# Seven-product feed-forward up-projection: PSUM copies issued ahead of the last pair's activations, another home for the first weights, one weight's subtraction on DVE

## The chip, the cores and the metric

The kernel runs on one core of one Trainium2 chip. The metric is the device time of the whole program in microseconds (us), median of three runs. Engines are named as in the profile: PE (TensorE matmuls) and PEld (its weight loads), DVE (VectorE), ACT (ScalarE), POOL (GpSimd), SP (SyncE, which here issues the loads). ACTq and SPq are DMA issues in the queues of ACT and SP.

## The reference

One decoder block: two token mixers, a merge, and a gated feed-forward with a convolution over three tokens. The change lies in the first half of the feed-forward, `h @ w_up`, the convolution and the gate; T = 1024 tokens, 1024 features, 2 x 2816 columns.

```python
def conv_ffn(h, w_up, conv_w, conv_b, w_down):
    u = h @ w_up
    T = u.shape[1]
    up = jnp.pad(u, ((0, 0), (CONV_WIDTH - 1, 0), (0, 0)))
    u = sum(up[:, i:i + T] * conv_w[i] for i in range(CONV_WIDTH)) + conv_b
    gate, val = jnp.split(u, 2, axis=-1)
    return (jax.nn.gelu(gate, approximate=True) * val) @ w_down
```

## The kernel before

The up-projection goes by 22 pairs of column tiles: a pair is 128 gate columns (weight tile j, channel b = 0) and the 128 value columns that they gate (tile j + 22, b = 1), for two halves of 512 tokens (hf = 0, 1). The first three pairs are made in the plain way by `up_std`. The other 19 (n = 0 to 18) are made by seven products of half the depth in place of eight: sums of weight halves times sums of input halves, put together after. Every product is three float32r terms (high x high, high x low, low x high) over four blocks of 128, so 12 matmuls of 512 columns; a pair is 84 matmuls. For the first four pairs (n < 4) two of the seven products are made ahead, in a stage called "e" here (lines 1108 to 1117), stored to DRAM (`e_s` to `e_d`) and loaded again; such a pair is 60 matmuls.

A pair's products in PE's order, with the PSUM tile: X1 (`ps_x`), Z1 (`ps_z`), T1 (`ps_t`), Y (`ps_y`), X2 (`ps_x`, accumulated onto X1), Z2 (`ps_z`, onto Z1), T2 (`ps_t`, onto T1). Between them: ACT copies X1 to `s1` (L1183) and Z1 to `s5` (L1188); DVE adds T1 into `s5` (L1190) and Y into `s1` (L1192); ACT copies X2 into `ub` (L1195), POOL adds `s1` and `s5` into `ub` (L1196), DVE adds Z2 (L1198) and T2 (L1200) with `s1` into `ub`. X2 may not start before the copy of X1, Z2 not before that of Z1, T2 not before the add of T1.

The weights of a pair: SP loads two tiles of 512 KB (`st1` L1148, `st2` L1150; both are `w_st` in the profile). DVE forms sums: `w_sa` (two operations, L1163 and L1164) and, in place, one half each of `st2` (L1166) and `st1` (L1167). `cut` makes of a weight its high part, a cast on ACT (L1159), and its low part, the weight minus the high part (L1160), on POOL for w1, w2 and w3 and on DVE for w4. w1 is cut from `st1`, w2 from `w_sa`, w3 from the two halves made in place, w4 from the untouched half of `st2`; the subtraction for w4 is the last reader of an `st2` buffer, of which there are two.

Then the convolution and the gate, for each token half: `conv` is one ACT operation (L1063) and two DVE operations (L1064, L1066) for each channel, `gate` a GELU on ACT (L1071), a product on DVE (L1072) and a store from ACT's queue (L1073).

Each engine works through its own queue in order. What order that is, a scheduler decides when the program is built, from the order of the code, from priorities (`tc.high_priority` for the weights) and from its own estimates. Weight buffers come from pools: `wp` lives from early on; `wx` and `fp` are opened when the "e" stage's pools (`b12`, `es`, `w3s`) are closed, in the same memory.

Of the kernel before, what the change touches and what calls it, by code (L numbers as in the profile page):

```python
# [9 lines left out]
F32 = mybir.dt.float32  # L10
F32R = mybir.dt.float32r
# [13 lines left out]
FT = 22  # L25
# [133 lines left out]
def body(tc, nc, xT, xN, pos, wch, wbrw, wbret, wout, wup, wdn, w2a2, gw2, rows, vecs, consts0, consts1, out):  # L159
    V, S, G, PE = nc.vector, nc.scalar, nc.gpsimd, nc.tensor  # L160
    ctx = ExitStack()

    @contextmanager
    def tile_pool(**kw):
        with tc.tile_pool(**kw) as pool:
            yield Lines(pool)

    with ctx:
# [30 lines left out]
        pool_lo = [False]  # L199
        wpools = [(wp, (2, 3, 2))]  # L200

        def load_w(src, kt, full=None, hi=None, lo=None, st=None):

            wp, nb = wpools[cnt[0] % len(wpools)]
            with tc.high_priority(offset=WPRIO if cnt[0] > 3 else 0):
                if st is None:
                    st = wp.tile([128, full or kt, 128], F32, tag="ws", name="w_st", bufs=nb[0])[:, 0:kt, :]
                nc.sync.dma_start(st, src)
            with tc.high_priority(offset=WPRIO if cnt[0] > 1 else 0):
                if hi is None:  # L210
                    hi = wp.tile([128, full or kt, 128], F32R, tag="wh", name="w_hi", bufs=nb[1])[:, 0:kt, :]
                S.copy(hi, st)  # L212
                if lo is None:
                    lo = wp.tile([128, full or kt, 128], F32R, tag="wl", name="w_lo", bufs=nb[2])[:, 0:kt, :]
                cnt[0] += 1
                eng = V if (cnt[0] % 3 == 0 and not pool_lo[0]) or cnt[0] < 3 else G
                eng.tensor_tensor(out=lo, in0=st, in1=hi, op=ALU.subtract)  # L217
            return hi, lo

# [819 lines left out]


        bp = ctx.enter_context(tile_pool(name="bp", bufs=1, reuse_waits="tile"))
        ectx = ExitStack()
        b12 = ectx.enter_context(tile_pool(name="b12", bufs=1, reuse_waits="tile"))
        es = ectx.enter_context(tile_pool(name="es", bufs=2, reuse_waits="tile"))

        w3s = ectx.enter_context(tile_pool(name="w3s", bufs=1, reuse_waits="tile"))
        wpools[:] = [(wp, (2, 3, 2)), (w3s, (1, 1, 1)), (wp, (2, 3, 2))]
        f_d = dp.tile([2, FT, 128, 512], F32, name="f_d")
        carry = cp.tile([128, 2 * NSTD, 2], F32, name="carry", bufs=1)
# [24 lines left out]

        def up_std(j, hf, late=False):
            cv = []
            ws = [load_w(wup[j + FT * b], 8) for b in range(2)]
            pss = [big("ps_up") for b in range(2)]
            if late:

                for b in range(2):
                    for k in range(8):
                        for z in range(2):
                            PE.matmul(pss[b], ws[b][z][:, k, :], hn2[hf][k][0], start=k + z == 0, stop=False)
                for b in range(2):
                    for k in range(8):
                        PE.matmul(pss[b], ws[b][0][:, k, :], hn2[hf][k][1], start=False, stop=k == 7)
            for b in range(2):
                w, ps = ws[b], pss[b]
                if not late:  # L1090
                    mm3(ps, [(w[0][:, k, :], w[1][:, k, :], hn2[hf][k][0], hn2[hf][k][1]) for k in range(8)])
                ub = es.tile([128, 514], F32, tag=f"ub{b}", name="ub")
                if hf == 0:
                    G.memset(ub[:, 0:2], 0.0)
                else:
                    G.tensor_copy(ub[:, 0:2], carry[:, 2 * j + b, :])
                S.copy(ub[:, 2:514], ps)
                if hf == 0:
                    G.tensor_copy(carry[:, 2 * j + b, :], ub[:, 512:514])
                cv.append(conv(es, ub, b, j, ps))  # L1100
            gate(j, hf, *cv)
# [6 lines left out]
        for n0 in range(0, NEAR, 2):  # L1108
            ws = [load_w(wup[NSTD + n], 8) for n in (n0, n0 + 1)]
            pss = [big("ps_e") for n in range(2)]  # L1110
            for z in range(2):
                for n in range(2):
                    mmb(pss[n], ws[n], range(4 * z, 4 * z + 4), hn2[0][4 * z:4 * z + 4], z == 0, True)
                    t = es.tile([128, 512], F32, tag=f"u{z}", name="e_s")
                    S.copy(t, pss[n])
                    nc.scalar.dma_start(e_d[n0 + n, z], t)
        up_std(0, 1, True)
# [24 lines left out]
        W8 = [128, 8, 128]  # L1142
        lh, rh_ = slice(0, 4), slice(4, 8)

        for n, j in enumerate(range(NSTD, FT)):
            with tc.high_priority(offset=WPRIO):
                st1 = wp.tile(W8, F32, tag="ws", name="w_st", bufs=2)
                nc.sync.dma_start(st1, wup[j])  # L1148
                st2 = wx.tile(W8, F32, tag="ws", name="w_st", bufs=2)
                nc.sync.dma_start(st2, wup[j + FT])  # L1150
                sa = wx.tile(W8, F32, tag="sa", name="w_sa")
                if n >= NEAR:
                    w1 = wp.tile(W8, F32R, tag="wh", name="w_hi", bufs=3), wx.tile(W8, F32R, tag="wl", name="w_lo", bufs=3)
                w2 = wx.tile(W8, F32R, tag="wh", name="w_hi", bufs=2), wx.tile(W8, F32R, tag="wl", name="w_lo", bufs=3)
                w3 = wp.tile(W8, F32R, tag="wh", name="w_hi", bufs=3), wp.tile(W8, F32R, tag="wl", name="w_lo", bufs=2)
                w4 = wx.tile(W8, F32R, tag="wh", name="w_hi", bufs=2), wp.tile(W8, F32R, tag="wl", name="w_lo", bufs=2)

                def cut(w, ks, src, eng):
                    S.copy(w[0][:, ks, :], src)  # L1159
                    eng.tensor_tensor(out=w[1][:, ks, :], in0=src, in1=w[0][:, ks, :], op=ALU.subtract)  # L1160
                if n >= NEAR:
                    cut(w1, slice(0, 8), st1, G)
                V.tensor_tensor(out=sa[:, lh, :], in0=st2[:, lh, :], in1=st2[:, rh_, :], op=ALU.add)  # L1163
                V.tensor_tensor(out=sa[:, rh_, :], in0=st1[:, lh, :], in1=st2[:, lh, :], op=ALU.subtract)  # L1164
                cut(w2, slice(0, 8), sa, G)
# [144 lines left out]
```

## Time and profile before

| | us |
|---|---|
| median of 3 runs | 1898.92 (1895.99 to 1899.91) |
| the profiled execution | 1902.93 |
| its span, first to last instruction | 1901.1 |
| the stretch from the "e" stage to the first product of n = 0 | about 1180 to 1254 |
| the seven-product stage, n = 0 to 18 | about 1254 to 1625 |

Times in the rows below are microseconds from the start of the span. A row of the timeline gives start, duration, engine, line, operation, tiles written and read, and in brackets how long the engine sat idle before it and what released it.

### The profile page before, as it was taken

The page shows a single profiled execution, that of the slowest core. Times are in us where ns is not written, and L with a number is a line of the kernel's source. Part 1 is how long each engine was busy: PE and PEld are TensorE (multiplying, and loading weights), DVE is VectorE, ACT ScalarE, POOL GpSimd, SP SyncE. Part 2 cuts the span into 40 slices and gives each one's busy share as a digit, 9 for nine tenths or more (in the row PEclk, how much of TensorE's full clock was granted, in tenths as well). Part 3 has the DMA queues.
Part 4 walks back from the last instruction along what each step waited for, and adds up shares of the span by engine and source line. Part 5 has one row for each costly group of instructions (what it writes and reads, how often), then busy time and mean ns, then how long its engine had stood idle before and what let it go on. Part 6 is the DMA issues. An engine that isn't in the chain of part 4 may idle for free.

```text
span 1901.1 us, 27394 instructions
## 1 busy us (share of the span) xinstructions
PE 1787.9 (94%) x10610; PEld 1450.2 (76%) x10610; DVE 1176.8 (62%) x2067; ACT 649.7 (34%) x993; POOL 686.1 (36%) x492
## 2 busy tenths in 40 slices
PE   8779999999999999999999999888999999999996
PEld 7657778788777778878788777666777777777885
DVE  4786584755666635663445828689888888752413
ACT  6543212111111112332443434544444444443320
POOL 1344523312212221111564744535454454222523
PEclk9989999999999999999999999899999999999998
DMA  8333532433333225455643735332222222664521
GB/s 285 87 113 100 191 83 67 134 90 94 109 100 105 69 89 176 151 177 172 217 154 123 242 106 197 122 135 89 89 67 78 83 73 78 221 210 142 188 92 44
DMA packets 202690, 244.44 MB, mean 129 GB/s; under 512 B 60992, under 2 KB 136256, under 8 KB 201536
## 3 DMA queue, kind: packets, MB, share of 16 engines
q1 hardware_dynamic: 125712, 171.11, 29.4%
q10 hardware_dynamic: 76848, 71.59, 11.5%
q8 instruction: 83, 1.36, 0.3%
q14 instruction: 47, 0.39, 0.1%
HBM read 177.10 MB, written 65.54 MB: 128 GB/s over the span
## 4 chain that ended last, share of the span: by engine, by line
PE 51%; DVE 17%; DMA 9%; issue 5%; ACT 4%; POOL 4%; ACTq 0%; SPq 0%; DVEq 0%; POOLq 0%
PE ps_side L224 7%; PE ps_side L223 7%; PE ps_side L225 7%; DVE u_f L1064 4%; PE ps_dn L225 3%; PE ps_dn L223 3%; PE ps_dn L224 3%; POOL w_lo L1160 2%; DMA w_st<-in_wup_dram 2%; DVE w_sa L1164 2%; DVE w_sa L1163 2%; PE ps_o L224 1%; PE ps_o L225 1%; PE ps_o L223 1%; DVE u_f L1066 1%
## 5 line engine op out<-in xcount | busy, mean ns | idle before, releaser
L217 POOL TENSOR_TENSOR w_lo<-w_st,w_hi 128x1024 fp32r<-128x1024 f32 (+2 forms) x112 | 272.4, 2433 | 513.6 <-ACT w_hi L212 183.8
L212 ACT CAST w_hi<-w_st 128x1024 fp32r<-128x1024 f32 (+2 forms) x162 | 161.7, 999 | 403.6 <-PE ps_side L224 125.8
L224 PE MATMUL ps_side<-hnl,w_hi 128*128 128x512 f32 x640 | 256.3, 400 | 0.0
L223 PE MATMUL ps_side<-hnh,w_hi 128*128 128x512 f32 x640 | 255.6, 399 | 0.0
L225 PE MATMUL ps_side<-hnh,w_lo 128*128 128x512 f32 x640 | 254.8, 398 | 0.0
L223 PEld LDWEIGHTS ps_side<-hnh,w_hi 128*128 128x128 f32 x640 | 121.1, 189 | 26.8 <-issue 1.5
L225 PEld LDWEIGHTS ps_side<-hnh,w_lo 128*128 128x128 f32 x640 | 121.1, 189 | 26.2 <-issue 0.8
L224 PEld LDWEIGHTS ps_side<-hnl,w_hi 128*128 128x128 f32 x640 | 121.0, 189 | 26.3 <-issue 1.5
L217 DVE TENSOR_TENSOR w_lo<-w_st,w_hi 128x1024 fp32r<-128x1024 f32 (+1 forms) x50 | 64.0, 1280 | 83.7 <-ACT w_hi L212 41.5
L1064 DVE SCALAR_TENSOR_TENSOR u_f<-ub,vct,u_f 128x512 f32<-128x512 f32 x88 | 105.5, 1204 | 13.9 <-ACT u_f L1063 13.8
L1160 POOL TENSOR_TENSOR w_lo<-w_st,w_hi 128x512 fp32r<-128x512 f32 (+1 forms) x53 | 106.0, 2024 | 0.0
L1063 ACT ACTIVATE u_f<-ub,vct 128x512 f32<-128x512 f32 x76 | 59.9, 812 | 129.2 <-DVE ub L1198 110.8
L223 PE MATMUL ps_rw<-hnh,w_hi 128*128 128x512 f32 (+1 forms) x224 | 87.8, 392 | 13.2 <-ACT hnh L288 7.0
L224 PE MATMUL ps_rw<-hnl,w_hi 128*128 128x512 f32 (+1 forms) x224 | 86.7, 387 | 0.7 <-DVE hnl L289 0.7
L225 PE MATMUL ps_rw<-hnh,w_lo 128*128 128x512 f32 (+1 forms) x208 | 80.0, 385 | 0.0
L225 PE MATMUL ps_b<-y_hi,w_lo 128*128 128x512 f32 x192 | 75.1, 392 | 1.9 <-DVE w_lo L217 1.2
L223 PE MATMUL ps_b<-y_hi,w_hi 128*128 128x512 f32 x192 | 75.2, 392 | 0.7 <-ACT w_hi L212 0.6
L224 PE MATMUL ps_b<-y_lo,w_hi 128*128 128x512 f32 x192 | 74.8, 390 | 0.0
L223 PE MATMUL ps_dn<-f_k,w_hi 128*128 128x512 f32 (+1 forms) x198 | 72.5, 366 | 0.0
L225 PE MATMUL ps_dn<-f_k,w_lo 128*128 128x512 f32 (+1 forms) x198 | 72.4, 367 | 0.0
L224 PE MATMUL ps_dn<-f_k,w_hi 128*128 128x512 f32 (+1 forms) x198 | 72.2, 366 | 0.0
L223 PE MATMUL ps_z<-b_hi,w_hi 128*128 128x512 f32 x152 | 60.4, 397 | 12.2 <-ACT w_hi L1159 8.0
(418 smaller groups left out, 4342.2 us busy)
## 6 DMA issues: line engine op xcount, KB each, us to landing
w_st<-in_wup_dram SPq DMA_DIRECT2D x54, 512.0 KB, 3.6
w_st<-in_wch_dram SPq DMA_DIRECT2D x52, 512.0 KB, 4.0
w_st<-in_wdn_dram SPq DMA_DIRECT2D x38, 512.0 KB, 4.0
pj_d<-ot ACTq DMA_DIRECT2D x64, 256.0 KB, 2.2
zvg<-pj_d SPq DMA_DIRECT2D x8, 1536.0 KB, 9.2
f_d<-u_f ACTq DMA_DIRECT2D x44, 256.0 KB, 2.1
L<-L_d SPq DMA_DIRECT2D x8, 1344.0 KB, 6.0
w_st<-in_wbret_dram SPq DMA_DIRECT2D x16, 512.0 KB, 3.7
```

Source lines behind the costliest of these rows:

```text
L212: S.copy(hi, st)
L217: eng.tensor_tensor(out=lo, in0=st, in1=hi, op=ALU.subtract)
L223: PE.matmul(ps, wh, xh, start=first and a == 0, stop=False, skip_group_check=skip)
L224: PE.matmul(ps, wh, xl, start=False, stop=False, skip_group_check=skip)
L225: PE.matmul(ps, wl, xh, start=False, stop=last and a == n - 1, skip_group_check=skip)
L1063: S.activation(u, src, AF.Identity, bias=VC("cb")[:, i:i + 1], scale=VC("cw2")[:, i:i + 1])
L1064: V.scalar_tensor_tensor(out=u, in0=ub[:, 1:513], scalar=VC("cw1")[:, i:i + 1], in1=u, op0=ALU.mult, op1=ALU.add)
L1066: V.scalar_tensor_tensor(out=u, in0=ub[:, 0:512], scalar=VC("cw0")[:, i:i + 1], in1=u, op0=ALU.mult, op1=ALU.add)
L1160: eng.tensor_tensor(out=w[1][:, ks, :], in0=src, in1=w[0][:, ks, :], op=ALU.subtract)
L1163: V.tensor_tensor(out=sa[:, lh, :], in0=st2[:, lh, :], in1=st2[:, rh_, :], op=ALU.add)
L1164: V.tensor_tensor(out=sa[:, rh_, :], in0=st1[:, lh, :], in1=st2[:, lh, :], op=ALU.subtract)
```

## The change

Line numbers move by 2 in `conv` and `gate` and by 5 to 11 in the pair loop; the prediction uses those of before.

1. `load_w` takes an engine for the low part; the second weight of `up_std(0, 1, True)`, the plain pair made last before the pair loop's inputs, has its subtraction on DVE in place of POOL.
2. `w3s` gets a life of its own and outlives the "e" stage. The pair n = 0 takes `st2`, `w_sa` and the low part of w2 from it, and the high parts of w2 and w4 from `wp`; every later even pair takes `w_sa` from it too, so `w_sa` has two buffers in place of one.
3. The `e_s` tiles for n = 1 take another tag, so the "e" stage has more buffers for them.
4. The convolution and the gate of a pair, all but the first ACT operation with its two DVE operations (channel 0, first half), become a function `rest()`, which is called in the next pair right after the copy of Z1, and so stand behind it in ACT's queue.

```diff
-                eng = V if (cnt[0] % 3 == 0 and not pool_lo[0]) or cnt[0] < 3 else G
+                if eng is None:
+                    eng = V if (cnt[0] % 3 == 0 and not pool_lo[0]) or cnt[0] < 3 else G
...
+        w3ctx = ExitStack()
+        w3s = w3ctx.enter_context(tile_pool(name="w3s", bufs=1, reuse_waits="tile"))
...
-        w3s = ectx.enter_context(tile_pool(name="w3s", bufs=1, reuse_waits="tile"))
...
-            ws = [load_w(wup[j + FT * b], 8) for b in range(2)]
+            ws = [load_w(wup[j + FT * b], 8, eng=V if late and b else None) for b in range(2)]
...
-                    t = es.tile([128, 512], F32, tag=f"u{z}", name="e_s")
+                    t = es.tile([128, 514], F32, tag=f"ub{z}" if n else f"u{z}", name="e_s")[:, 0:512]
...
-                st2 = wx.tile(W8, F32, tag="ws", name="w_st", bufs=2)
+
+                st2 = wx.tile(W8, F32, tag="ws", name="w_st", bufs=2) if n else w3s.tile(W8, F32, tag="ws", name="w_st")
...
-                sa = wx.tile(W8, F32, tag="sa", name="w_sa")
+                sa = (wx.tile(W8, F32, tag="sa", name="w_sa") if n % 2 else
+                      w3s.tile(W8, F32, tag="wh", name="w_sa"))
...
-                w2 = wx.tile(W8, F32R, tag="wh", name="w_hi", bufs=2), wx.tile(W8, F32R, tag="wl", name="w_lo", bufs=3)
+                wh = (wx, 2) if n else (wp, 3)
+                w2 = (wh[0].tile(W8, F32R, tag="wh", name="w_hi", bufs=wh[1]),
+                      wx.tile(W8, F32R, tag="wl", name="w_lo", bufs=3) if n else w3s.tile(W8, F32R, tag="wl", name="w_lo"))
...
-            S.copy(s5, pZ)
+
+            with tc.issue_after(S.copy(s5, pZ).ins):
+                rest()
...
-            for hf in range(2):
-                cv = [conv(fp, ub[b][:, 512 * hf:512 * hf + 514], b, j, ub[b][:, 512 * hf + 2:512 * hf + 514])
-                      for b in range(2)]
-                gate(j, hf, *cv)
+
+            def part(b, hf, j=j, ub=ub):
+                return conv(fp, ub[b][:, 512 * hf:512 * hf + 514], b, j, ub[b][:, 512 * hf + 2:512 * hf + 514])
+
+            def rest(j=j, part=part, u0=part(0, 0)):
+                gate(j, 0, u0, part(1, 0))
+                gate(j, 1, part(0, 1), part(1, 1))
+        rest()
```

How the queues stand before and after, at three places. ACT, one pair of the steady part, before; the pair's own activations end it, and the two copies for the next pair stand behind them:

```order
L1183 COPY s1_12297<-ps_x_12289 128x512
L1188 COPY s5_12298<-ps_z_12290 128x512
...
L1159 CAST w_hi_12420<-w_sa_12417 128x1024
...
L1195 COPY ub_12293<-ps_x_12289 128x512
L1063 ACTIVATE u_f_12391<-ub_12293,vct_76 128x512
...
L1063 ACTIVATE u_f_12402<-ub_12293,vct_76 128x512
L1071 ACTIVATE u_f_12391<-u_f_12391 128x512
...
L1063 ACTIVATE u_f_12395<-ub_12294,vct_76 128x512
L1063 ACTIVATE u_f_12406<-ub_12294,vct_76 128x512
L1071 ACTIVATE u_f_12402<-u_f_12402 128x512
L1183 COPY s1_12448<-ps_x_12440 128x512
```

ACT, one pair of the steady part, of the change; between the copy of Z1 and the cast of the next pair's w2 now stand four operations on the last pair's `ub` and `u_f`:

```order
L1192 COPY s1_12429<-ps_x_12421 128x512
L1198 COPY s5_12430<-ps_z_12422 128x512
L1065 ACTIVATE u_f_12457<-ub_12275,vct_76 128x512
L1073 ACTIVATE u_f_12390<-u_f_12390 128x512
L1065 ACTIVATE u_f_12464<-ub_12274,vct_76 128x512
L1065 ACTIVATE u_f_12468<-ub_12275,vct_76 128x512
L1168 CAST w_hi_12552<-w_sa_12549 128x1024
L1075 DMA f_d_10242<-u_f_12390 128x512
L1073 ACTIVATE u_f_12464<-u_f_12464 128x512
L1168 CAST w_hi_12554<-w_st_12547 128x512
...
L1192 COPY s1_12580<-ps_x_12572 128x512
```

DVE, the same part, before, from a pair's add of T1 to the next add of T2; nine operations and more stand between the subtraction for w4 (`w_lo_12123`) and the next `w_sa`:

```order
L1200 TENSOR_TENSOR ub_11992<-ps_t_11989,s1_11995 128x512
L1066 SCALAR_TENSOR_TENSOR u_f_12100<-ub_11991,vct_76,u_f_12100 128x512
L1160 TENSOR_TENSOR w_lo_12123<-w_st_12113,w_hi_12122 128x512
L1064 SCALAR_TENSOR_TENSOR u_f_12093<-ub_11992,vct_76,u_f_12093 128x512
L1167 TENSOR_TENSOR w_st_12262<-w_st_12262,w_st_12264 128x512
...
L1190 TENSOR_TENSOR s5_12147<-ps_t_12140,s5_12147 128x512
L1192 TENSOR_TENSOR s1_12146<-ps_y_12141,s1_12146 128x512
L1163 TENSOR_TENSOR w_sa_12417<-w_st_12415 128x512
L1164 TENSOR_TENSOR w_sa_12417<-w_st_12413,w_st_12415 128x512
```

DVE of the change, one pair whole; `w_sa` stands two operations behind the subtraction for w4, and its input `w_st_13453` is loaded into the buffer that this subtraction read (`w_st_13151`):

```order
L1211 TENSOR_TENSOR ub_13030<-ps_t_13027,s1_13033 128x512
L1169 TENSOR_TENSOR w_lo_13161<-w_st_13151,w_hi_13160 128x512
L1176 TENSOR_TENSOR w_st_13300<-w_st_13300,w_st_13302 128x512
L1172 TENSOR_TENSOR w_sa_13455<-w_st_13453 128x512
L1173 TENSOR_TENSOR w_sa_13455<-w_st_13451,w_st_13453 128x512
L1175 TENSOR_TENSOR w_st_13453<-w_sa_13455,w_st_13451 128x512
L1066 SCALAR_TENSOR_TENSOR u_f_13212<-ub_13030,vct_76,u_f_13212 128x512
L1068 SCALAR_TENSOR_TENSOR u_f_13212<-ub_13030,vct_76,u_f_13212 128x512
L1066 SCALAR_TENSOR_TENSOR u_f_13219<-ub_13029,vct_76,u_f_13219 128x512
L1201 TENSOR_TENSOR s5_13185<-ps_t_13178,s5_13185 128x512
...
L1203 TENSOR_TENSOR s1_13184<-ps_y_13179,s1_13184 128x512
```

Behind these come, in the same pair, L1068 of the second half's value channel, the product L1074, L1066, L1209 (Z2), L1068, and the next L1211. In POOL's queue the order of the change is the low part of w1 (one pair ahead of w2), of w2, the add of `s1` and `s5`, and the two halves of w3; before, the same ring starts with w2.

ACT ahead of the first pair n = 0, before (`ps_up` are plain pairs, `w_sa_11023` is of n = 0), then of the change; the cast of w2 stood behind two stores and GELUs of plain pairs and now stands right behind the first read of `ps_up_10942`:

```order
L1063 ACTIVATE u_f_10971<-ps_up_10942,vct_76 128x512
L1097 COPY ub_10999<-ps_up_10943 128x512
L1063 ACTIVATE u_f_11002<-ps_up_10943,vct_76 128x512
L1073 DMA f_d_10242<-u_f_10892 128x512
L1071 ACTIVATE u_f_10971<-u_f_10971 128x512
L1159 CAST w_hi_11024<-w_sa_11023 128x1024
```

```order
L1075 DMA f_d_10242<-u_f_10741 128x512
L1073 ACTIVATE u_f_10892<-u_f_10892 128x512
L960 CAST b_hi_10847<-t_4_10829 128x512
L1065 ACTIVATE u_f_10971<-ps_up_10942,vct_76 128x512
L1168 CAST w_hi_11023<-w_sa_11022 128x1024
L1099 COPY ub_10999<-ps_up_10943 128x512
```

The counts of instructions stay, but for the one subtraction that goes from POOL to DVE. Behind the pair loop the program is as before, but for a small reordering of loads.

## Rows read from the trace of the kernel before

**Rows 1.** PE's waits between 1100 and 1680 us: total, times, longest.

```profile
PE ps_x L223 <- ACT s L1183: 16.8, 14, 2.1
PE ps_z L223 <- ACT w_hi L1159: 8.0, 1, 8.0
PE ps_up L225 <- POOL w_lo L217: 5.9, 1, 5.9
PE ps_e L223 <- ACT e_s L1115: 4.1, 2, 3.3
```

**Rows 2.** One steady pair by window: length, then busy time of PE, PEld, DVE, ACT, POOL.

```profile
1454.86:1475.36 20.50, 19.33 (x84) 15.69 (x84) 17.46 (x20) 9.18 (x15) 10.06 (x7) 1.00 0.23 77
```

**Rows 3.** PE's timeline: start of Z1 and of X2 in the steady part.

```profile
1446.00 0.39 PE L223 MATMUL ps_z<-b_hi,w_hi 128*128 128x512 f32 x1
...
1455.48 0.50 PE L223 MATMUL ps_x<-b_hi,w_hi 128*128 128x512 f32 x1 [1.15 <-ACT s L1183]
```

**Rows 4.** ACT's timeline, the same pair.

```profile
1450.68 0.82 ACT L1063 ACTIVATE u_f<-ub,vct 128x512 f32<-128x512 f32 x1 [7.80 <-DVE ub L1198]
...
1452.92 1.52 ACT L1063 ACTIVATE u_f<-ub,vct 128x512 f32<-128x512 f32 x2 [0.39 <-DVE ub L1200]
1454.34 0.61 ACT L1071 ACTIVATE u_f<-u_f 128x512 f32<-128x512 f32 x1
1454.86 0.56 ACT L1183 COPY s<-ps_x 128x512 f32<-128x512 f32 x1
```

**Rows 5.** DVE's timeline, the same pair.

```profile
1452.20 0.69 DVE L1200 TENSOR_TENSOR ub<-ps_t,s 128x512 f32<-128x512 f32 x1
1452.80 0.74 DVE L1066 SCALAR_TENSOR_TENSOR u_f<-ub,vct,u_f 128x512 f32<-128x512 f32 x1
1453.46 0.68 DVE L1160 TENSOR_TENSOR w_lo<-w_st,w_hi 128x512 fp32r<-128x512 f32 x1
...
1462.57 1.77 DVE L1163 TENSOR_TENSOR w_sa<-w_st 128x512 f32<-128x512 f32 x1 [2.78 <-POOL w_lo L1160]
1464.27 1.77 DVE L1164 TENSOR_TENSOR w_sa<-w_st 128x512 f32<-128x512 f32 x1
```

**Rows 6.** POOL's timeline, the same pair.

```profile
1460.13 2.41 POOL L1160 TENSOR_TENSOR w_lo<-w_sa,w_hi 128x1024 fp32r<-128x1024 f32 x1 [2.52 <-ACT w_hi L1159]
1462.50 1.29 POOL L1196 TENSOR_TENSOR ub<-s,s 128x512 f32<-128x512 f32 x1
1463.75 6.24 POOL L1160 TENSOR_TENSOR w_lo<-w_st,w_hi 128x512 fp32r<-128x512 f32 x3
```

**Rows 7.** Loads and stores issued between 1440 and 1482: KB each, median us to landing.

```profile
w_st<-in_wup_dram SPq DMA_DIRECT2D x4, 512.0 KB, 3.6
```

**Rows 8.** DVE's timeline at the last pairs: POOL's next row starts at 1611.69.

```profile
1611.56 0.75 DVE L1066 SCALAR_TENSOR_TENSOR u_f<-ub,vct,u_f 128x512 f32<-128x512 f32 x1
1612.36 2.77 DVE L1064 SCALAR_TENSOR_TENSOR u_f<-ub,vct,u_f 128x512 f32<-128x512 f32 x1
```

**Rows 9.** POOL's timeline, there and where DVE runs without a gap.

```profile
1206.97 12.66 POOL L217 TENSOR_TENSOR w_lo<-w_st,w_hi 128x1024 fp32r<-128x1024 f32 x1 [6.47 <-PE ps_e L225]
...
1611.69 2.89 POOL L217 TENSOR_TENSOR w_lo<-w_st,w_hi 128x1024 fp32r<-128x1024 f32 x1 [1.97 <-ACT w_hi L212]
```

**Rows 10.** ACT's timeline between the "e" stage and n = 0, and a later copy of Z1.

```profile
1188.82 0.58 ACT L1115 COPY e_s<-ps_e 128x512 f32<-128x512 f32 x1 [6.64 <-DMA e_d<-e_s]
...
1247.62 0.78 ACT L1063 ACTIVATE u_f<-ps_up,vct 128x512 f32<-128x512 f32 x1 [3.98 <-DMA f_d<-u_f]
...
1252.45 1.04 ACT L1159 CAST w_hi<-w_sa 128x1024 fp32r<-128x1024 f32 x1 [1.29 <-DVE w_sa L1164]
...
1332.45 0.57 ACT L1188 COPY s<-ps_z 128x512 f32<-128x512 f32 x1
```

**Rows 11.** All copies of Z1, one for each pair: count, durations, first and last start.

```profile
L1188 ACT COPY s<-ps_z x19: 559/579/587, 1263.9 to 1618.7; 128x512 f32<-128x512 f32 x19
```

**Rows 12.** By window (columns as above, then the granted clock).

```profile
1189.20:1196.00 6.80, 6.54 (x17) 5.15 (x18) 0.07 (x1) 3.72 (x6) 0.27 (x1) 0.56 0.60 193
```

More of the change, by code (lines that the diff above doesn't have):

```diff
@@ L200, in body, with load_w @@
         wpools = [(wp, (2, 3, 2))]
-        def load_w(src, kt, full=None, hi=None, lo=None, st=None):
+        def load_w(src, kt, full=None, hi=None, lo=None, st=None, eng=None):
             wp, nb = wpools[cnt[0] % len(wpools)]
@@ L1143, in body, with rest @@
         lh, rh_ = slice(0, 4), slice(4, 8)
+        def rest():
+            pass
         for n, j in enumerate(range(NSTD, FT)):
@@ L1148, in body @@
                 nc.sync.dma_start(st1, wup[j])
-                st2 = wx.tile(W8, F32, tag="ws", name="w_st", bufs=2)
+                st2 = wx.tile(W8, F32, tag="ws", name="w_st", bufs=2) if n else w3s.tile(W8, F32, tag="ws", name="w_st")
                 nc.sync.dma_start(st2, wup[j + FT])
-                sa = wx.tile(W8, F32, tag="sa", name="w_sa")
+                sa = (wx.tile(W8, F32, tag="sa", name="w_sa") if n % 2 else
+                      w3s.tile(W8, F32, tag="wh", name="w_sa"))
                 if n >= NEAR:
                     w1 = wp.tile(W8, F32R, tag="wh", name="w_hi", bufs=3), wx.tile(W8, F32R, tag="wl", name="w_lo", bufs=3)
-                w2 = wx.tile(W8, F32R, tag="wh", name="w_hi", bufs=2), wx.tile(W8, F32R, tag="wl", name="w_lo", bufs=3)
+                wh = (wx, 2) if n else (wp, 3)
+                w2 = (wh[0].tile(W8, F32R, tag="wh", name="w_hi", bufs=wh[1]),
+                      wx.tile(W8, F32R, tag="wl", name="w_lo", bufs=3) if n else w3s.tile(W8, F32R, tag="wl", name="w_lo"))
                 w3 = wp.tile(W8, F32R, tag="wh", name="w_hi", bufs=3), wp.tile(W8, F32R, tag="wl", name="w_lo", bufs=2)
-                w4 = wx.tile(W8, F32R, tag="wh", name="w_hi", bufs=2), wp.tile(W8, F32R, tag="wl", name="w_lo", bufs=2)
+                w4 = wh[0].tile(W8, F32R, tag="wh", name="w_hi", bufs=wh[1]), wp.tile(W8, F32R, tag="wl", name="w_lo", bufs=2)
                 def cut(w, ks, src, eng):
@@ L1200, in body @@
             V.tensor_tensor(out=ub[1][:, 2:514], in0=pT, in1=s1, op=ALU.add)
-            for hf in range(2):
-                cv = [conv(fp, ub[b][:, 512 * hf:512 * hf + 514], b, j, ub[b][:, 512 * hf + 2:512 * hf + 514])
-                      for b in range(2)]
-                gate(j, hf, *cv)
+            def part(b, hf, j=j, ub=ub):
[4 more added lines that the diff above has]
+        rest()
         fctx.close()
+        w3ctx.close()
         n2 = ctx.enter_context(tile_pool(name="n2", bufs=2, reuse_waits="tile", side="right"))
```

## The prediction

> **What bounds the kernel now.** I read PE's waits first, then a steady pair in windows, then the timelines of ACT, DVE and POOL in that pair, and last the copies of Z1, which give every pair's period.
>
> PE's costliest wait between 1100 and 1680 us is X2 on the copy `s1` of X1: 14 times, 16.8 us [rows 1]. X1 had ended by 1446.00, where Z1 starts, yet the copy ran at 1454.86, and X2 started at 1455.48 [rows 3, 4]. ACT's row tells why: the copy stands behind the last pair's activations, and those waited 7.80 us for DVE's add of Z2 [rows 4]. A pair takes (1618.7 - 1332.45) / 14 = 20.45 us [rows 10, 11]. PE alone needs less: 36 matmuls (Z1, T1, Y) from 1446.00 to 1455.48 less the idle 1.15 are 8.33 us [rows 3], of which 0.16 is the end of the last one, so 0.227 each and 19.05 for 84. Each far pair thus loses 1.4 us.
>
> What sets the 20.45? The sum of DVE's and POOL's work, not ACT's 9.18 [rows 2]. `w_sa` beside POOL takes 1.77 where a like operation alone takes 0.68 [rows 5], and an STT 2.77 in place of 0.75 while POOL has a row [rows 8, 9]: an operation of one waits for one of the other. I call what they share the port. Spacings: DVE 0.60 for a TT (1452.20 to 1452.80), 0.66 for an STT (1452.80 to 1453.46) [rows 5]; POOL 1.25 for 512 columns, 2.37 for 1024 [rows 6]; one of DVE and a short one of POOL in turn 1.70 (1462.57 to 1464.27) [rows 5]. A pair has 7 TT and 8 STT without PSUM on DVE (9.5 us), 4 TT that read PSUM (2.4), and on POOL three short and two long operations (8.5).
>
> Who gets the port? POOL's subtraction at 1206.97 took 12.66 us in a stream of DVE [rows 9]: it doesn't get in between operations 0.60 apart. But at 1611.69 it asked and did get in: the two STTs there start 0.80 apart (1611.56 and 1612.36) where 0.66 is usual, and the second took 2.77 [rows 8, 9]. So I take it that POOL gets in where DVE has a small gap, as between an operation and the next that needs its result.
>
> **The copies ahead of the activations.** This removes the wait for `s1`: up to 1.4 us for each of 14 pairs, 19.6 in all, if nothing else is late. What is late next has to be read from the new queues, taken from one add of T2, for pair Q, to the next. Time 0 is the start of that add.
>
> DVE: the subtraction for w4 ends at about 1.3. It frees the buffer into which the next `st2` is loaded, and `w_sa` two operations behind needs that load, which lands 3.6 us later [rows 7], at 4.9. Before, nine and more operations stood between. Meanwhile ACT goes through an activation of Q (0.72 after the add's start, as from 1452.20 to 1452.92), a GELU (0.52, 1454.34 to 1454.86) and two more activations (each 0.71) [rows 4, 5], all ahead of the cast of the next w2 (1.04) [rows 10]: 0.72 + 3 x 0.71 + 0.52 + 1.04 = 4.4. So neither DVE nor POOL has anything for the port from about 1.9 to 4.4: **2.5 us are lost**, where before a pair lost next to nothing, since w2's subtraction lay beside DVE's 2.78 us of waiting [rows 5, 6]. At 4.4 POOL starts w2's subtraction, half a microsecond ahead of the load, and holds `w_sa` up to 6.8.
>
> Then DVE runs 11 operations up to the add of Y, 6 x 0.60 + 5 x 0.66 + 0.12 for a pair in which one needs the other = 7.0, to 13.8; POOL's next, the add of `s1` and `s5`, waits for the last of them. One STT more, 14.5. The product behind it needs its result, so POOL gets in. From here in turn: POOL's add and the product 1.70; a half of w3 1.25 (DVE waits for ACT's activation behind the store of that product); the other half and an STT 1.75; w1's subtraction 2.37 and the last STT 0.5. That is 22.1, and there the next add of T2 starts. T1's add is then late and PE waits ahead of T2. I take **22.0 a pair**; 21.4 if one turn more lies beside a PSUM operand of DVE, 22.7 if operations that follow one another don't overlap. Against 20.45 that is (22.0 - 20.45) x 14 = **+21.7** (13 to 31).
>
> Near pairs (n < 4) took (1332.45 - 1263.9) / 4 = 17.1 [rows 10, 11]. Without w1 the same chain gives 22.0 - 2.4 = 19.6, but the first starts with nothing queued: **+3** (0 to 10).
>
> **First weights, and the "e" stage.** The cast of w2 for n = 0 ran at 1252.45 and PE waited 8.0 us for it [rows 1, 10]. It now follows the activation that ended at 1247.62 + 0.78 = 1248.40, for which ACT waited on a store; 1252.45 - 1248.40 = 4.05 earlier. The activation's own wait stays, hence **-4** (0, if `w_sa` isn't ready, to -8). With more `e_s` buffers the copy at 1188.82, which waited 6.64 for a store [rows 10], can start when PE is done. PE's waits there are 4.1 [rows 1], and behind them 17 matmuls took 6.80 at a granted clock of 0.56 [rows 12], against 17 x 0.227 = 3.9: up to 7 us. The other tag's tiles still wait, so **-5** (0 to -7). A POOL subtraction held up by DVE for 12.66 us, for which PE waits 5.9 [rows 1, 9], belongs to another weight than the one that goes to DVE, so that wait stays. The moved subtraction costs DVE about 1.2 (two of 0.60 for twice the columns) in a place where it waits for PE: **0** (bounds: +1.2 if that cover is gone, -2.4 if the time it frees on POOL is all on PE's path).
>
> **Sum.** +21.7 + 3 - 4 - 5 = +15.7 on the profiled execution's 1902.93: 1918.6. The median of the runs is 4.0 lower, so **1914**. Its own range: 13 + 0 - 15 - 2 to 31 + 10 + 1, from 1895 to 1941; within that I hold 1902 to 1930 likely.
>
> **A rule weighed.** The Trainium skill (SBUF — State Buffer, "SBUF: two separate sides") calls the port pair of VectorE and GpSimd an exclusive lock: whoever starts first keeps it for the whole instruction, and the other blocks. The rows of 1.77 and 2.77 agree. Taken alone it makes a pair the sum of the locked work, 9.5 + 8.5 = 18.0 us, under PE's 19.05, and the change would reach PE's bound, the second rival's 1867. The row of 20.45 speaks against using the sum so: it is 2.4 above 18.0 in the kernel before, where the port is hardly ever without a taker.
>
> **Rivals.** First, *DVE stays ahead of POOL in the last part*. If the product goes ahead of POOL's add, w1's 2.37 falls behind the add of T2, beside the wait for the load, and costs nothing: 22.1 - 2.4 = 19.7, say 19.8. Far pairs -0.65 x 14 = -9, near 0, the rest -9: -18, so 1881. For it: the stream at 1206.97. Against it: the row at 1611.69. The point that decides is who has the port right after the STT behind the add of Y.
>
> Second, *PE's bound*. The load is shorter or the wait is covered, and pairs take 19.1: -1.35 x 14 = -19, near pairs -4, the rest -9: -32, so 1867. For it: PE needs T1's add only when Z2 is done, some 8 us after T1, so one pair can be late without loss. Against it: that slack is used once, and a ring of 22 us repeats.
>
> Third, *the reordering does nothing on balance*: 21.0 to 21.3 a pair, and the +8 to +12 are paid by the -9 of the first weights: 1898 to 1902; or pairs stay at 20.45, as DVE and POOL do the same work, and only the -9 is left: 1890.
>
> **Chances.** Forecast 0.54, first rival 0.24, second 0.12, third 0.10. Faster or slower by over 0.2% (3.8 us) is about what a measurement of this kernel can tell. Of the forecast's 0.54, 0.05 lie within it and 0.01 below; the third rival gives 0.03 within and 0.07 below. Faster 0.24 + 0.12 + 0.07 + 0.01 = 0.44, same 0.08, slower 0.48. Cases of both signs hold most of the chance, so the range goes from 1874, between the first and second rival, to 1930, which leaves out the second rival and the forecast's upper tail.
>
> **What would show it.** X2's wait for `s1` gone, which I hold for sure. Then: PE waiting ahead of T2 for DVE's add of T1; `w_sa` (L1172) idle some 3 us ahead of itself, released by a load; POOL idle ahead of w2's subtraction with ACT's cast as releaser; copies of Z1 about 22 apart. If they are 19.1 apart and PE waits for nothing, the ring is wrong. I am wrong in the first rival's way if w1's subtraction starts behind the add of T2. In the first part: the cast of n = 0's w2 some 4 us nearer the last plain pair, and the row at 1188.82 without a wait for a store.

## The result, and the profile after

The changed kernel takes 1916.96 us (median of 4 runs, 1915.67 to 1918.03), the kernel before 1899.41; the ratio is 1.0087, 95% interval 1.0066 to 1.0107. The prediction was 1914, slower. The profiled execution took 1918.03 us with a span of 1916.2.

PE's waits between 1100 and 1680 us, the four longest and some behind them (total, times, longest), beside [rows 1]:

```profile
PE ps_t L224 <- DVE s L1201: 28.0, 13, 3.9
PE ps_up L226 <- POOL w_lo L218: 5.8, 1, 5.8
PE ps_z L224 <- ACT s L1198: 5.4, 1, 5.4
PE ps_z L226 <- POOL ub L1187: 3.1, 1, 3.1
...
PE ps_z L226 <- POOL w_lo L1169: 2.6, 1, 2.6
PE ps_y L226 <- POOL w_lo L1169: 1.5, 1, 1.5
PE ps_z L224 <- ACT w_hi L1168: 1.2, 1, 1.2
...
PE ps_e L224 <- ACT e_s L1117: 0.2, 1, 0.2
```

The 14 waits for the copy of X1 are gone. In their place PE waits 13 times ahead of T2 for DVE's add of T1, 28.0 us in all; the waits for the copy were 16.8. The waits for the first cast (8.0) and for `e_s` (4.1) have shrunk to 1.2 and 0.2. In the near pairs PE waits more for POOL than before: 3.1, 2.6 and 1.5 us, where the trace before has one such wait, of 1.2.

Two steady pairs by window, cut at the start of the add of T2 (columns as in [rows 2], the granted clock behind POOL):

```profile
1454.23:1476.30 22.07, 19.32 (x78) 15.42 (x77) 17.56 (x21) 8.95 (x14) 9.98 (x7) 0.92 0.23 71
1476.30:1498.39 22.09, 20.99 (x93) 17.07 (x92) 17.72 (x20) 9.40 (x15) 9.99 (x7) 1.00 0.23 72
```

A pair takes 22.08. DVE and POOL are as busy as before [rows 2], so the 1.6 us by which a pair is longer went into idle time. DVE's timeline shows where, over one pair:

```profile
1476.30 0.68 DVE L1211 TENSOR_TENSOR ub<-ps_t,s 128x512 f32<-128x512 f32 x1
1476.90 0.68 DVE L1169 TENSOR_TENSOR w_lo<-w_st,w_hi 128x512 fp32r<-128x512 f32 x1
1477.50 0.68 DVE L1176 TENSOR_TENSOR w_st<-w_st 128x512 f32<-128x512 f32 x1
1481.06 2.71 DVE L1172 TENSOR_TENSOR w_sa<-w_st 128x512 f32<-128x512 f32 x1 [2.88 <-DMA w_st<-in_wup_dram]
1483.70 0.68 DVE L1173 TENSOR_TENSOR w_sa<-w_st 128x512 f32<-128x512 f32 x1
...
1489.65 0.69 DVE L1203 TENSOR_TENSOR s<-ps_y,s 128x512 f32<-128x512 f32 x1
1490.26 0.75 DVE L1068 SCALAR_TENSOR_TENSOR u_f<-ub,vct,u_f 128x512 f32<-128x512 f32 x1
1491.11 1.60 DVE L1074 TENSOR_TENSOR u_f<-u_f 128x512 f32<-128x512 f32 x1
1494.02 1.64 DVE L1066 SCALAR_TENSOR_TENSOR u_f<-ub,vct,u_f 128x512 f32<-128x512 f32 x1 [1.31 <-ACT u_f L1065]
1495.58 0.68 DVE L1209 TENSOR_TENSOR ub<-ps_z,s 128x512 f32<-128x512 f32 x1
1496.18 2.29 DVE L1068 SCALAR_TENSOR_TENSOR u_f<-ub,vct,u_f 128x512 f32<-128x512 f32 x1
1498.39 0.68 DVE L1211 TENSOR_TENSOR ub<-ps_t,s 128x512 f32<-128x512 f32 x1
```

`w_sa` waits 2.88 for its load, and then, once ready, takes 2.71 in place of 0.68 since POOL has started. POOL's timeline, the same pair:

```profile
1480.83 2.40 POOL L1169 TENSOR_TENSOR w_lo<-w_sa,w_hi 128x1024 fp32r<-128x1024 f32 x1 [5.00 <-ACT w_hi L1168]
...
1490.42 1.74 POOL L1207 TENSOR_TENSOR ub<-s,s 128x512 f32<-128x512 f32 x1 [0.52 <-DVE s L1203]
...
1492.16 5.76 POOL L1169 TENSOR_TENSOR w_lo<-w_st,w_hi 128x512 fp32r<-128x512 f32 x3
```

POOL sits idle 5.00 us for ACT's cast of w2, and starts 0.23 ahead of the moment at which `w_sa` could. From 1478.2 to 1480.8 neither works. At 1490.42 POOL's add asks while DVE is in an STT (a SCALAR_TENSOR_TENSOR), and it goes ahead of the product that needs that STT's result (1491.11, which takes 1.60 for 0.68). All three of w3 and w1 are through by 1497.9, ahead of the next add of T2. ACT's timeline, with the four activations between the copy and the cast:

```profile
1475.93 0.59 ACT L1198 COPY s<-ps_z 128x512 f32<-128x512 f32 x1 [2.10 <-PE ps_z L226]
1477.01 0.82 ACT L1065 ACTIVATE u_f<-ub,vct 128x512 f32<-128x512 f32 x1 [0.49 <-DVE ub L1211]
1477.74 0.61 ACT L1073 ACTIVATE u_f<-u_f 128x512 f32<-128x512 f32 x1
1478.26 1.51 ACT L1065 ACTIVATE u_f<-ub,vct 128x512 f32<-128x512 f32 x2
1479.67 1.03 ACT L1168 CAST w_hi<-w_sa 128x1024 fp32r<-128x1024 f32 x1
```

### The profile page after: what moved, and what is told of

It is laid out like the page before. It is cut to its first block, busy times and chain, and to the rows that moved or that the text cites. A ratio compares the mean times of both kernels' runs of the same rounds, so it can differ in the third digit from the quotient of the medians.

```text
span 1916.2 us, 27335 instructions
## 1 busy us (share of the span) xinstructions
PE 1796.7 (94%) x10610; PEld 1457.0 (76%) x10610; DVE 1182.8 (62%) x2068; ACT 649.4 (34%) x993; POOL 689.5 (36%) x491
## 4 chain that ended last, share of the span: by engine, by line
PE 48%; DVE 22%; DMA 10%; issue 4%; POOL 3%; ACT 2%; ACTq 0%; SPq 0%; DVEq 0%; POOLq 0%
PE ps_side L225 6%; PE ps_side L224 6%; PE ps_side L226 6%; DVE u_f L1066 4%; DVE u_f L1068 3%; PE ps_dn L226 3%; PE ps_dn L225 3%; PE ps_dn L224 3%; DMA w_st<-in_wup_dram 2%; DVE w_sa L1172 2%; DVE u_f L1074 2%; PE ps_o L225 1%; PE ps_o L226 1%; PE ps_o L224 1%; DVE xprod L628 1%
## 5 line engine op out<-in xcount | busy, mean ns | idle before, releaser
L218 POOL TENSOR_TENSOR w_lo<-w_st,w_hi 128x1024 fp32r<-128x1024 f32 (+2 forms) x111 | 261.4, 2355 | 512.6 <-ACT w_hi L212 164.0
L1066 DVE SCALAR_TENSOR_TENSOR u_f<-ub,vct,u_f 128x512 f32<-128x512 f32 x88 | 90.2, 1028 | 33.3 <-ACT u_f L1065 28.7
L1169 POOL TENSOR_TENSOR w_lo<-w_st,w_hi 128x512 fp32r<-128x512 f32 (+1 forms) x53 | 100.3, 1917 | 3.4 <-ACT w_hi L1168 1.9
L1068 DVE SCALAR_TENSOR_TENSOR u_f<-ub,vct,u_f 128x512 f32<-128x512 f32 x88 | 95.7, 1090 | 0.7
L224 PE MATMUL ps_t<-b_hi,w_hi 128*128 128x512 f32 x152 | 64.0, 421 | 28.0 <-DVE s L1201 28.0
L1169 POOL TENSOR_TENSOR w_lo<-w_sa,w_hi 128x1024 fp32r<-128x1024 f32 x19 | 50.7, 2667 | 100.2 <-ACT w_hi L1168 93.9
L1065 ACT ACTIVATE u_f<-ub,vct 128x512 f32<-128x512 f32 x76 | 59.8, 810 | 50.4 <-DVE u_f L1074 20.1
L1073 ACT ACTIVATE u_f<-u_f 128x512 f32<-128x512 f32 x44 | 27.6, 626 | 140.2 <-DVE u_f L1068 140.2
```

Of the source, the lines that this page charges most:

```text
L224: PE.matmul(ps, wh, xh, start=first and a == 0, stop=False, skip_group_check=skip)
L1065: S.activation(u, src, AF.Identity, bias=VC("cb")[:, i:i + 1], scale=VC("cw2")[:, i:i + 1])
L1066: V.scalar_tensor_tensor(out=u, in0=ub[:, 1:513], scalar=VC("cw1")[:, i:i + 1], in1=u, op0=ALU.mult, op1=ALU.add)
L1068: V.scalar_tensor_tensor(out=u, in0=ub[:, 0:512], scalar=VC("cw0")[:, i:i + 1], in1=u, op0=ALU.mult, op1=ALU.add)
L1073: S.activation(u0, u0, AF.Gelu_apprx_tanh)
```

## Where the time went

To compare stretches I count from PE's first "e" product (1171.38 before, 1169.20 after). Over the thirteen traces here, one for each kernel, it starts between 1164.4 and 1174.4. From it, the first Z1 of n = 0 and the adds of T2 in the pairs n = 4 and 18 start as follows (1253.55, 1349.40 and 1631.31 in the trace before, 1237.15, 1343.78 and 1645.85 after).

| us after the first "e" product | first Z1 | n = 4 | n = 18 | pair, n = 6 to 16 |
|---|---|---|---|---|
| before | 82.2 | 178.0 | 459.9 | 20.51 |
| the change | 68.0 | 174.6 | 476.6 | 22.09 |
| e1: without the deferral | 67.6 | 171.8 | 433.5 | 18.88 |
| e2: the deferral alone | 78.5 | 176.7 | 446.6 | 19.50 |
| e3: third `st2` buffer | 64.1 | 164.5 | 428.2 | 18.91 |
| e4: cast ahead of activations | 68.2 | 169.8 | 441.9 | 19.53 |
| e5: first part undone | 68.0 | 174.2 | 476.6 | 22.11 |
| e6: both mends | 67.9 | 169.4 | 430.6 | 18.66 |
| e7: no deferral, third buffer | 67.3 | 168.6 | 429.4 | 18.97 |
| e8: no deferral, one `w_sa` | 67.7 | 165.6 | 447.8 | 20.54 |
| e9: `w_sa` later on DVE | 67.3 | 166.1 | 431.2 | 19.01 |
| e10: no deferral, old `e_s` | 73.1 | 176.8 | 440.0 | 19.02 |
| e11: no deferral, n = 0 in `wx` | 74.1 | 170.7 | 437.0 | 19.09 |

Where PE is busy all the time (e1, e3, e6, e7) a pair is 19.0 by its matmuls; the last column goes by DVE's adds, which drift against PE, and can be a little less.

Up to the first Z1 the change gains 14.2. PE has as many matmuls there as before and does them in 4.1 us less, at a higher granted clock, and it is idle for 10.2 us less (before, then after; columns as above):

```profile
1171.38:1253.55 82.17, 63.15 (x257) 50.37 (x255) 59.44 (x93) 38.67 (x62) 34.73 (x15) 0.89 0.46 153
1169.20:1237.15 67.95, 59.09 (x258) 47.41 (x256) 54.59 (x87) 37.00 (x60) 35.12 (x15) 0.95 0.50 163
```

From there to the add of T2 in n = 4 it loses 106.63 - 95.85 = 10.8. PE's waits in that stretch, without the one ahead of the first Z1, grow from 8.1 to 16.7 us. The wait of 3.1 that the profile puts down to `ub` on POOL ends with a subtraction for w2 that stood ahead of it and took 5.25 in place of 2.40:

```profile
1249.83 5.25 POOL L1169 TENSOR_TENSOR w_lo<-w_sa,w_hi 128x1024 fp32r<-128x1024 f32 x1 [3.58 <-ACT w_hi L1168]
1255.03 0.20 POOL L1187 MEMSET ub<- 128x2 f32 x4
```

The last 14 pairs lose 302.1 - 281.9 = 20.2. Together that is +16.7, and +0.6 behind the last add. The 2.2 by which the first "e" product itself is earlier is not of the change as far as these runs show.

## The experiments

All ratios are to the kernel before on the same chip.

**e1: without the fourth part.** `rest()` goes, the loop over `hf` at the pair's end comes back.

```diff
-            with tc.issue_after(S.copy(s5, pZ).ins):
-                rest()
+            S.copy(s5, pZ)
```

> The change without its fourth part: the convolution and gate are issued at the pair's own end again, all else as in the change. My theory (the loss comes from the deferred activations, which put the cast of w2 and the load both late): the early parts keep their gain, the first copy of Z1 near 1253 in place of 1264 and the first add of T2 some 7 us earlier than before; far pairs are as before, 20.0 to 20.6 a pair, with PE waiting ahead of X2 for the copy of X1. About 1889 to 1894. Rival (the loss comes from the second w_sa buffer and the pool moves, which reorder DVE): far pairs stay near 22 and the time near 1915.

Measured: 1875.8, ratio 0.9878 (0.9845 to 0.9912). So the first three parts gain 24 us and the fourth costs some 40 on top of them. My theory's side held, but the pair fell to PE's bound, not to 20.0 to 20.6: PE is busy all the time (the window's columns as above). Its 972 matmuls in 220.00 us are 0.226 each, 19.0 a pair, as the prediction worked out (19.05).

```profile
1360.00:1580.00 220.00, 220.00 (x972) 182.19 (x971) 179.55 (x223) 112.08 (x163) 113.05 (x82) 1.00 0.26 86
```

The load is still a little late there, since `w_sa` stands six operations behind the subtraction for w4 and not two:

```profile
1460.67 0.69 DVE L1172 TENSOR_TENSOR w_sa<-w_st 128x512 f32<-128x512 f32 x1 [0.34 <-DMA w_st<-in_wup_dram]
```

**e2: the fourth part alone,** on the kernel before; the diff is the last piece of the change.

> The kernel before with the fourth part alone: one w_sa buffer, so w_sa has to follow the subtraction for the last w2 and stands ten DVE operations further behind the subtraction for w4, and the load is covered; the cast of w2 still stands behind four activations. My theory: part of the idle port is filled; the ring is 12.1 us of DVE operations plus what POOL blocks (2.2 for w2, 1.1 for the add and for each half of w3, 2.2 for w1) = 19.8, about 20.0 a pair with small waits; the first pairs as before (first copy of Z1 near 1264). About 1892 to 1898. Rival (the order of the activations alone makes the pair 22, whatever the load does): 22 a pair, about 1920.

Measured: 1885.01, ratio 0.9930 (0.9907 to 0.9953), 19.50 a pair. By itself the deferral gains nearly 15 us. That is better than the forecast of 1892 to 1898. It costs some 40 only where `w_sa` has two buffers.

**e8: without the fourth part, one `w_sa` buffer.**

```diff
-                sa = (wx.tile(W8, F32, tag="sa", name="w_sa") if n % 2 else
+                sa = (wx.tile(W8, F32, tag="sa", name="w_sa") if n else
```

> The change without its fourth part and with one w_sa buffer for the pairs after n = 0: the queues of the steady pair are then those of the kernel before. Theory: the second w_sa buffer is what took the far pair from 20.45 to 19.05, since it lets w_sa go ahead of the subtraction for the last w2; with one buffer 20.45 comes back, PE waits for the copy of X1 again, and only the early part's gain is left: 1886 to 1892. Rival: the pool moves or the head start did it, and the pair stays at 19.05: about 1876.

Measured: 1888.79, ratio 0.9951 (0.9931 to 0.9971), 20.54 a pair, as the theory had it. The wait for the copy of X1 is back, and behind it the reason: with one buffer `w_sa` waits for POOL's subtraction for the last w2, 2.8 us a pair (eleven pairs from 1360 to 1580), as in the kernel before; e1 has no such wait.

```profile
PE ps_x L224 <- ACT s L1192: 16.1, 14, 1.4
...
DVE w_sa L1172 <- POOL w_lo L1169: 30.9, 11, 3.0
```

So the early parts by themselves give 0.5%, some 9 us, and the second `w_sa` buffer another 14. With e1, e2 and the change this fills a table of two by two, for the far pair: neither 20.5, deferral alone 19.5, second `w_sa` buffer alone 19.0, both 22.1. (e2 also lacks the early parts; before and e8, without and with them, have the same pair.)

**e3: a third `st2` buffer,** in the change.

```diff
-                st2 = wx.tile(W8, F32, tag="ws", name="w_st", bufs=2) if n else w3s.tile(W8, F32, tag="ws", name="w_st")
+                st2 = wx.tile(W8, F32, tag="ws", name="w_st", bufs=2) if n % 3 else w3s.tile(W8, F32, tag="ws", name="w_st")
```

> The change with a third buffer for st2 (every third pair takes the tile that only n = 0 used), so that the load of the next st2 no longer waits for the subtraction for w4. The cast of w2 stays behind the four activations. My theory: w_sa no longer waits for a load; w2's subtraction at 4.4 now lies inside DVE's run and costs it about 2.3 there: 1.9 + 6.4 + 2.3 + 8.9 = 19.5 a pair, about 1877 to 1884. Rival one (the load alone is the loss): 19.05, PE's bound, about 1872. Rival two (the late cast alone is the loss): still near 22, about 1915.

Measured: 1867.95, ratio 0.9840 (0.9812 to 0.9869), PE busy all the time between 1360 and 1580. Of the 29.7 us for which DVE waited for loads 0.3 are left. That reads as rival one, but e4 shows that the cast counts too. The run also doesn't tell the buffer from the order: the scheduler also moved the first of the two `w_sa` operations ahead of the subtraction for w4 (1459.79 and 1466.29).

**e4: the cast ahead of the activations,** in the change. The pair's weights are traced one pair earlier, so that the cast can be named; from the second pair on their priority is also lowered by 60, in lines not shown.

```diff
+            c5 = S.copy(s5, pZ).ins
+            nxt = weights(n + 1) if n + NSTD + 1 < FT else None
-            with tc.issue_after(S.copy(s5, pZ).ins):
+            with tc.issue_after(nxt[4] if nxt else c5):
                 rest()
```

> The change with the deferred activations queued behind the cast of the next pair's w2, which makes ACT's queue copy, copy, cast, activations; the load stays exposed. My theory: w2's subtraction lies beside the wait for the load, POOL runs from 1.2 to 3.6, w_sa starts when the load lands at 4.9 and the rest of the ring is 15.2: 20.1 a pair, less if the earlier adds of T1 and Y let POOL start sooner; about 1884 to 1892. Rival one (the load alone): still near 22, about 1915. Rival two (the late cast alone): 19.05, about 1872.

Measured: 1880.96, ratio 0.9907 (0.9881 to 0.9932), 19.53 a pair. Of the wait for the load under a third is left over the eleven pairs between 1360 and 1580 (it was 29.7 in ten):

```profile
DVE w_sa L1175 <- DMA w_st<-in_wup_dram: 9.8, 11, 3.0
...
1458.80 2.29 DVE L1171 TENSOR_TENSOR w_lo<-w_st,w_hi 128x512 fp32r<-128x512 f32 x1
1461.01 2.89 DVE L1179 TENSOR_TENSOR w_st<-w_st 128x512 f32<-128x512 f32 x1
1464.36 0.69 DVE L1175 TENSOR_TENSOR w_sa<-w_st 128x512 f32<-128x512 f32 x1 [0.46 <-DMA w_st<-in_wup_dram]
...
1460.50 2.85 POOL L1171 TENSOR_TENSOR w_lo<-w_sa,w_hi 128x1024 fp32r<-128x1024 f32 x1
```

The load has not become shorter: `w_sa` starts 3.3 us behind the end of the subtraction for w4 (1461.09). But POOL now has w1's and w2's subtractions at that time, so the two DVE operations ahead of `w_sa` take 2.29 and 2.89 in place of 0.68, and w2's is through before `w_sa` starts.

So each mend alone removes most of the loss. That fits two gaps that overlap: DVE waits for a load while POOL waits for a cast, and it is enough to fill one. In e3 and e9 (below) the cast still stands behind the four activations, and with the load in time it costs nothing.

**e6: both mends.**

> The change with both mends: three st2 buffers and the cast of w2 ahead of the deferred activations. If the late load and the late cast are the whole loss, and each mend alone has already taken the pair to 19.5 and to PE's bound of 19.05, both together stay at 19.05: 1866 to 1874, as with three buffers alone. If something else of the deferred order costs (the adds' place, the stores), a wait of PE for DVE's add of T1 is left and it is above 1874.

Measured: 1866.2, ratio 0.9842 (0.9806 to 0.9877); PE waits for nothing between 1360 and 1580. This and e3 are the fastest versions here, 30 to 32 us under the kernel before.

**e9: `w_sa` later in DVE's queue.** Buffers and ACT's queue stay as in the change; `sy` holds each pair's add of Y.

```diff
-                V.tensor_tensor(out=sa[:, lh, :], in0=st2[:, lh, :], in1=st2[:, rh_, :], op=ALU.add)
-                V.tensor_tensor(out=sa[:, rh_, :], in0=st1[:, lh, :], in1=st2[:, lh, :], op=ALU.subtract)
+                with (tc.issue_after(sy[n - 2]) if n > 1 else ExitStack()):
+                    V.tensor_tensor(out=sa[:, lh, :], in0=st2[:, lh, :], in1=st2[:, rh_, :], op=ALU.add)
+                    V.tensor_tensor(out=sa[:, rh_, :], in0=st1[:, lh, :], in1=st2[:, lh, :], op=ALU.subtract)
```

> The change with the two w_sa operations of a pair queued on DVE behind the add of Y two pairs earlier, in place of right behind the subtraction for w4. Buffers and ACT's queue stay as in the change, the cast of w2 behind the four activations too; DVE's steady queue is then that of the run with the fourth part alone (19.50 a pair). Theory (the load is late only because w_sa stands two operations behind the subtraction that frees its buffer): 19.4 to 19.6 a pair, no wait for a load ahead of w_sa, 1876 to 1886. Rival (the second w_sa buffer or the pools cost by themselves): 22 a pair, about 1915.

Measured: 1870.43, ratio 0.9859 (0.9834 to 0.9885). Moving two DVE operations back by eight places takes some 43 us away, more than forecast. DVE no longer waits for a load, and it is busy, the time that POOL holds it up included, for nearly 19 us in a pair of 19.0:

```profile
1412.64:1431.65 19.01, 19.01 (x86) 15.74 (x85) 18.98 (x21) 9.20 (x14) 10.30 (x7) 1.00 0.26 84
```

**e5: the first part undone,** `eng=None` for the late weight.

> The change with its first part undone: the plain pair's second weight is subtracted on POOL again. Theory: the moved subtraction lies where DVE waits for PE and POOL is not the last for that weight, so nothing moves, 1917 within 3. Rival: the time it frees on POOL is on PE's path, and undoing it costs 2 to 6, 1919 to 1923.

Measured: 1911.26, ratio 1.0082 (1.0053 to 1.0110). The ratio is the change's, and the stretches agree within 0.5 us: the part moves nothing that can be measured.

**e7: no deferral, third buffer.**

> The change without its fourth part, and with three st2 buffers. Without the deferral the far pairs were at PE's bound already, 19.05, with 0.34 us of waiting for the load that no one waited for in turn. Theory: the third buffer gives nothing there, 1876 within 3. Rival: the three buffers gave 8 us in the run of the change with them by other means than the far pairs (the wait of 5.5 us for POOL in the plain pairs was gone there), and do so here: 1866 to 1871.

Measured: 1872.42, ratio 0.9867 (0.9832 to 0.9901). The interval holds e1's ratio; whether the third buffer gives a few microseconds there stays open.

**e10 and e11: the early parts, one run each,** both without the fourth part. e10 takes the old `e_s` tags back, e11 loads n = 0's weights into `wx` again.

> The change without its fourth part and with the old e_s tags (third part undone as well), one look. Theory: PE's wait of 3 to 4 us for e_s is back, with a stretch of half clock behind it, and the first add of T2 is 4 to 7 us later than with the new tags (1261 to 1273 in the looks so far). Rival: another wait in that stretch takes the time anyway, and it moves by under 2.

> The change without its fourth part and with the weights of n = 0 in the late pool again (the second w_sa buffer for even pairs stays), one look. Theory: st2 of n = 0 is loaded late, the cast of its w2 stands behind the last plain pair's activations, and PE's wait of 8 us ahead of the first Z1 is back where it was 1.2; the first add of T2 is 3 to 6 us later. Rival: the n = 0 weights are as early as before and the gain comes from the e_s tags alone: under 2 later.

Measured: e10 1887.79, e11 1868.36, one run each, so their stretches say more than their times. In e10 PE's wait for `e_s` is back; the first Z1 is 73.08 - 67.56 = 5.5 later than in e1, and the add of T2 in n = 0 is later by 5.6. In e11 the wait ahead of the first Z1 is back (e10's wait, then e11's):

```profile
PE ps_e L224 <- ACT e_s L1117: 3.0, 1, 3.0
...
PE ps_z L224 <- ACT w_hi L1168: 5.7, 1, 5.7
```

The first Z1 of e11 is 74.12 - 67.56 = 6.6 later than e1's. Its add of T2 in n = 0 is not later (99.1 and 99.7 behind the first "e" product), but that is not the same point of PE's work: from the first Z1 up to it PE has 77 matmuls in e11 and 97 in e1, where first products of n = 1 go ahead. By n = 18 e11 is 3.5 behind e1, so about half of the early start is kept.

## Why the prediction was right, and where it was off

**The ring.** The prediction made a pair 22.0 out of rows of the kernel before; it is 22.08. Its steps stand in the timeline: `w_sa` idle 2.88 for a load (forecast some 3), POOL idle until a cast behind four activations (w2's subtraction 4.53 behind the start of the add of T2, forecast 4.4), `w_sa` held up to 6.8 or so (it ends at 1483.77, 7.47 behind, forecast 6.8 + 0.6), the add of Y at 13.35 (13.2), and POOL's three last subtractions ahead of the next add of T2. The far pairs cost 20.2, forecast 21.7.

**Who gets the port.** The first rival hung on this. POOL's add asked behind the add of Y and got in ahead of the product, as at 1611.69 in [rows 8, 9]. The first rival's sign, w1's subtraction behind the add of T2, isn't there. The reading that this rested on, that POOL gets in only where DVE leaves a small gap, the runs do not bear out as a rule. In e9 POOL asks at 1455.19 and is in ahead of a DVE operation that follows the one before by 0.60:

```profile
1455.16 0.69 DVE L1074 TENSOR_TENSOR u_f<-u_f 128x512 f32<-128x512 f32 x1
1455.76 2.89 DVE L1066 SCALAR_TENSOR_TENSOR u_f<-ub,vct,u_f 128x512 f32<-128x512 f32 x1
...
1455.19 2.90 POOL L1171 TENSOR_TENSOR w_lo<-w_sa,w_hi 128x1024 fp32r<-128x1024 f32 x1 [5.02 <-ACT w_hi L1170]
```

What kept POOL out for some 10 us at 1206.97 stays open.

**The rule.** The sum of the locked work alone would make a pair 18.0, and PE the bound. The Trainium skill (SBUF — State Buffer, "SBUF: two separate sides") calls the port pair an exclusive lock. e9 isn't at odds with that: once no one waits for a load, DVE and POOL fit into 19.0. In the change, for 2.6 us a pair nobody asked for the lock, and 22.1 less 2.6 is about the 19.5 of e2 and e4.

**Off: what the deferral removes.** The prediction took the late copy of X1 for the thing to remove, 1.4 us a pair. The copy was late because the ring of DVE and POOL was; e1 and e8 show that the second `w_sa` buffer removes that wait with ACT's queue unchanged. The prediction priced that buffer only by what it moved, not by what it would do alone.

**Off: the near pairs, and the first weights.** The step that was mis-sized is the near pairs: +3 (0 to 10) forecast, +10.8 measured from the first Z1 to the add of T2 in n = 4. The prediction looked there only for a longer chain behind the deferral. The traces show PE waiting more for POOL's low parts, for the copy of Z1 and for the add of T1, and most of that comes without the deferral: the stretch is 97.9 in e8 and 104.3 in e1, which has a second `w_sa` buffer besides, and 106.6 in the change.

The first weights gave more than the -9 forecast (-4 for the cast, -5 for `e_s`): -14.2 at the first Z1, within the 0 to -15 that was allowed. e10 puts 5.5 on `e_s` and e11 6.6 on the weights of n = 0; before and e2, alike in these parts, lie 3.7 apart there, so a difference of two traces is no better than that. Of their signs, the cast stands right behind the activation, whose own wait for a store fell from 3.98 to 0.28; a copy to `e_s` still waits for a store, though PE hardly waits for it (0.2):

```profile
1185.07 0.59 ACT L1117 COPY e_s<-ps_e 128x512 f32<-128x512 f32 x1 [4.38 <-DMA e_d<-e_s]
...
1235.38 0.78 ACT L1065 ACTIVATE u_f<-ps_up,vct 128x512 f32<-128x512 f32 x1 [0.28 <-DMA f_d<-u_f]
1236.06 1.03 ACT L1168 CAST w_hi<-w_sa 128x1024 fp32r<-128x1024 f32 x1
```

So the near pairs cost 7.8 more than forecast, the first weights gave 5.2 more, the far pairs cost 1.5 less, the part behind the last add took 0.6 more, and the stretch began 2.2 earlier: 15.7 + 7.8 - 5.2 - 1.5 + 0.6 - 2.2 = 15.2, and the two profiled executions differ by 15.1. That the sum came out so near is luck in part: the two largest errors have opposite signs. The medians differ by 17.6.

**Off: what the ring costs once a gap is filled.** The same chain gave 20.0 for e2 and 20.1 for e4, and both runs gave 19.5. It gave 19.5 for e3 and 19.4 to 19.6 was expected of e9; both ended at PE's bound, so of their ring only that it is no longer than 19.0 is known. The chain came out right where everything waits in turn, and too long elsewhere, perhaps because POOL and DVE then find each other's PSUM operations and waits to hide in; no run tests that.

## What to carry to other kernels

Two edits that each gain can lose together: here a second buffer let an operation move up in its queue to right behind the instruction that frees its input's buffer, and a deferral gave the partner engine nothing to do in that same stretch. Where two engines exclude each other, look at stretches in which neither works, not at either's busy share. And read, in the new queues, how many instructions stand between the last reader of a load's buffer and the first user of the load: here a distance of two left 2.9 us of the load uncovered, six left 0.3, and ten left nothing.

## What the runs showed of the hardware that was not expected

PE's wait ahead of T2 alternates from pair to pair between 2.75 and 1.10 us, and the granted clock with it: 0.92 in the one window shown above and 1.00 in the next, the copies of Z1 alternately 20.4 and 23.7 apart (1452.20, 1475.93, 1496.36, 1520.09), while DVE's ring keeps 22.07 and 22.09. Behind the wait of 2.75, which ends at 1465.79, the clock falls to 0.50, the lower of its two levels (1.2 GHz):

```profile
1468.00:1470.00 2.00, 2.00 (x6) 1.51 (x6) 1.90 (x3) 1.84 (x4) 1.66 (x1) 0.50 0.00 0
```

The pair gets no longer by it: DVE's ring sets the period there.

The stretch ahead of the first "e" product, which the edits don't touch but for small reorderings, differs by up to 10 us between traces of these kernels. A comparison of two traces by absolute times would have given the early parts 2.2 us too much.
